# Six weight buffers at six start addresses, and the high weights of two contraction blocks multiplied first

## The chip, the cores and the metric

The kernel runs on one core of one Trainium2 chip. The metric is the device time of one execution in microseconds (us); 899.43 us is the median of two runs before the change (899.22 and 899.65). One execution was also taken with the hardware profiler, and all durations below come from it.

## The reference

A decoder trunk of two layers over 256 positions with a model width of 2048, all in float32. What matters for the time are its large projections:

```python
def ab_layer(h, w_in, gla_w_gate, gla_b_gate, gla_norm_g, w_out):
    z = h @ w_in                                  # 2048 x 7184
    ...                                           # dilated attention, 8 heads; gated linear attention, 4 heads
    y = jnp.concatenate([ya, yb], axis=-1) * jax.nn.silu(gate)
    return y @ w_out                              # 2048 x 2048

def cd_layer(h, w_in, ...):
    z = h @ w_in                                  # 2048 x 6144
    yc = s5_mixer(...)                            # state space, with y * sigmoid(y @ w_glu + b_glu), 1024 x 1024
    ...                                           # gated recurrence, 8 heads
    y = jnp.concatenate([yc, yd], axis=-1) * jax.nn.silu(gate)
    return y @ w_out                              # 2048 x 2048

for l in range(2):
    h = h + layer(rmsnorm(h, norm_g[l]))          # ab_layer, then cd_layer
return rmsnorm(h, final_g)
```

## The kernel before

**Splitting.** Each float32 operand of a projection is split into a high part, rounded to the matrix engine's reduced form (float32r), and a low part, the remainder. A product is then three products: high weights with high activations, high weights with low activations, low weights with high activations. The activations of a layer's input stand in `xh` and `xl` (2048 x 256 as 16 blocks of 128 rows), those ahead of an output projection in `yh` and `yl`.

**Weights.** All weights stream through once. `load_split` (line 143) fetches a group of four contraction blocks by 512 columns, 1 MB, into one of three `raw` buffers over SP's DMA queue. Each half of it, a pair of contraction blocks, is split: ScalarE (ACT) writes `wh` (line 168), VectorE (DVE) writes `wl` as raw minus wh (line 169). `wh` and `wl` have three buffers each, and each buffer holds one pair, 4,096 bytes per partition. Both operations are marked urgent, so the scheduler puts them ahead of the other work of their engines.

**Products.** `gemm_fm` (line 173) gives the result with features on the partitions: a weight block of 128 x 128 is loaded into the array (the stationary operand), and 256 activation columns are streamed past it (the moving operand); four such matmuls for the four column blocks of the weights, at line 181. `gemm_tm` (line 192) gives it with positions on the partitions: 128 activation columns are stationary, 512 weight columns are moving, two matmuls, at line 200. Both accumulate over 16 contraction blocks in `pg` in PSUM, and both go block by block: for one contraction block all three products, then the next block. The last quarter of the last projection has a loop of its own (line 756) over the same kind of buffers.

**Order.** The program gives the order in which work is recorded; a scheduler orders each engine's instructions at build time by a simulated timeline and priorities. It puts the product with the low activations second, ahead of the one with the low weights. Small matmuls of the attention and the recurrences are set between those of the projections; `hook` (line 134) puts pieces of the state-space layer behind the matmuls of a pair.

**Addresses.** Tiles are laid out in the order of their pools and sizes. `ones`, a small constant, is taken 56 columns wider than it is used, which moves everything behind it in memory.

Of the kernel before, what the change touches and what calls it, by code (L numbers as in the profile page):

```python
# [12 lines left out]
F32 = mybir.dt.float32  # L13
F32R = mybir.dt.float32r
# [6 lines left out]
S = 256  # L21
# [36 lines left out]
def trunk(ctx: ExitStack, tc: tile.TileContext, I, out):  # L58
    nc = tc.nc
    V, G, A, T = nc.vector, nc.gpsimd, nc.scalar, nc.tensor  # L60

    const = ctx.enter_context(tc.tile_pool(name="const", bufs=1))
    stream = ctx.enter_context(tc.tile_pool(name="stream", bufs=6))
# [8 lines left out]
    def urgent():  # L72
        return tc.high_priority(offset=HI)
# [6 lines left out]
    oT = const.tile([128, KT, S], F32, name="oT")  # L80
    cst = const.tile([128, NCST], F32, name="cst")
    msk = const.tile([128, len(LV), 32], I32, name="msk")
    ones = const.tile([128, 128 + 56], F32, name="ones")[:, 0:128]
    sqa = const.tile([128, 4, S], F32, name="sqa")
    ident = cst[:, C_ID:C_ID + 128]

# [3 lines left out]
    def pm_tile(name="pm"):  # L90
        return pm.tile([128, 512], F32, name=name, tag="pm")
# [40 lines left out]
    state = {"mm": None, "wh": None, "first": True}  # L132
    fillq = []

    def hook():
        if fillq:
            todo = fillq.pop(0)
            if todo:
                with tc.issue_after(state["mm"].ins):
                    for fn in todo:  # L140
                        fn()

    def load_split(src, g):
        raw = stream.tile([128, 4, 512], F32, name="raw", bufs=3)
        first = state["first"]
        state["first"] = first and g < 3
        with urgent():
            if first:
                for a, b in ((0, 1), (1, 2), (2, 3), (3, 4)) if g == 0 else ((0, 2), (2, 4)):
                    xs = slice(NV + (4 * g + a) * S if g + a else 0, NV + (4 * g + b) * S)  # L150
                    load(xv[:, xs], I["xv"][:, xs])
                    for c in (slice(0, 256), slice(256, 512)) if g + a == 0 else (slice(0, 512),):
                        load(raw[:, a:b, c], src[g][:, a:b, c])
                for kt in range(4 * g, 4 * g + 4):
                    split_x(kt, V_NG0)
            else:
                state["load"] = nc.sync.dma_start(raw, src[g])
        if first and g == 3:
            load_consts()
        for half in range(2):  # L160
            wh = stream.tile([128, 2, 512], F32R, name="wh", bufs=3)
            wl = stream.tile([128, 2, 512], F32R, name="wl", bufs=3)
            with urgent():
                for a, b, c, d in (((0, 1, 0, 256), (0, 1, 256, 512), (1, 2, 0, 512)) if first and g == 0
                                   else ((0, 2, 0, 512),)):
                    r = raw[:, 2 * half + a:2 * half + b, c:d]
                    w, l = wh[:, a:b, c:d], wl[:, a:b, c:d]
                    state["wh"] = A.activation(w, r, AF.Copy)  # L168
                    V.tensor_sub(l, r, w)  # L169
            for k in range(2):  # L170
                yield 4 * g + 2 * half + k, wh[:, k], wl[:, k]
            hook()

    def gemm_fm(src, groups, ah, al, mid=None, order=None):
        ps = pg.tile([128, 4, S], F32, name="pg")
        last = groups * 4 - 1
        for i, kt, wh, wl in _iter(src, groups, mid, order):
            for n, (w, a) in enumerate(((wh, ah), (wh, al), (wl, ah))):
                for c in range(4):
                    cs = slice(c * 128, (c + 1) * 128)  # L180
                    state["mm"] = T.matmul(ps[:, c], w[:, cs], a[:, kt],  # L181
                                           start=(i == 0 and n == 0 and c % 2 == 0),
                                           stop=(i == last and n == 2), skip_group_check=True)
        return ps

    def _iter(src, groups, mid, order):
        for n, g in enumerate(order or range(groups)):
            for m, (kt, wh, wl) in enumerate(load_split(src, g)):
                yield 4 * n + m, kt, wh, wl
            if mid and 2 * (n + 1) == groups:  # L190
                mid()

    def gemm_tm(src, groups, ah, al, mid=None, order=None):
        ps = pg.tile([128, 2, 512], F32, name="pg")
        last = groups * 4 - 1
        for i, kt, wh, wl in _iter(src, groups, mid, order):
            for n, (w, a) in enumerate(((wh, ah), (wh, al), (wl, ah))):
                for t in range(2):
                    ts_ = slice(t * 128, (t + 1) * 128)
                    state["mm"] = T.matmul(ps[:, t], a[:, kt, ts_], w, start=(i == 0 and n == 0),  # L200
                                           stop=(i == last and n == 2), skip_group_check=True)
        return ps

    def split_x(kt, go):
# [35 lines left out]
    f, q, k = gla_tiles()  # L240
# [135 lines left out]
    for h0 in range(0, 4, 2):  # L376
        ps = pm_tile().rearrange("p (n s) -> p n s", n=2)
# [160 lines left out]
    sp_ = sp.enter_context(tc.tile_pool(name="s5", bufs=1))  # L538
# [3 lines left out]
    for b in range(2):  # L542
        ps = gemm_fm(w1[b], 4, xh, xl)
# [8 lines left out]
    def s5_quarter(qt):  # L552
        t = {}
# [75 lines left out]
            return go  # L629

        def finish():
            ys = sp_.tile([128, 8, 64], F32, name="ys")
            A.activation(ys, t["py"], AF.Copy)
            for g in range(2):
                for s in range(4):
                    (nc.gpsimd if s % 2 else nc.scalar).dma_start(
                        yv[g, s][:, 8 * qt:8 * qt + 8], ys[g * 64 + s * 16:g * 64 + s * 16 + 16])
            yc = sp_.tile([128, 2, S], F32, name="yc")
            nc.gpsimd.dma_start(yc, s5_y[256 * qt:256 * qt + 256].rearrange("(j p) f -> p j f", p=128))
            gw = sp_.tile([128, 2, S], F32, name="gw")  # L640
            A.activation(gw, yc, AF.Square)
            A.activation(gw, gw, AF.Copy, scale=0.044715, bias=1.0)
            V.tensor_mul(gw, gw, yc)
            A.activation(gw, gw, AF.Tanh, scale=math.sqrt(2.0 / math.pi))
            A.activation(yc, yc, AF.Copy, scale=0.5)
            for n in range(2):
                V.scalar_tensor_tensor(oT[:, 2 * qt + n].rearrange("p (c s) -> p s c", s=4),
                                       gw[:, n].rearrange("p (s c) -> p s c", s=4), 1.0,
                                       yc[:, n].rearrange("p (s c) -> p s c", s=4), op0=OP.add, op1=OP.mult)
# [11 lines left out]
    for half in range(2):  # L661
        f, q, k = gla_tiles()
# [24 lines left out]
    for b in range(2):  # L687
        ps = gemm_fm(I["wg"][b], 2, yh[:, 8:16], yl[:, 8:16])
# [35 lines left out]
    part = const.tile([128, 2], F32, name="part")  # L724
# [18 lines left out]
    for b in range(3):  # L743
        res, h2 = residual(b)
        ps = gemm_tm(I["wo1"][b], 4, yh, yl, order=(2, 3, 0, 1))
# [4 lines left out]
    for half in range(2):  # L750
        ps = pg.tile([128, 2, 512], F32, name="pg")

        def mms(kt, t, w, l):
            ts_ = slice(t * 128, (t + 1) * 128)
            for n, (w_, a_) in enumerate(((w, yh), (w, yl), (l, yh))):
                T.matmul(ps[:, t, 0:256], a_[:, kt, ts_], w_, start=(kt == 0 and n == 0),  # L756
                         stop=(kt == KT - 1 and n == 2), skip_group_check=True)

        for g in range(2):
            raw = stream.tile([128, 8, 256], F32, name="raw", bufs=3)  # L760
            with urgent():
                nc.sync.dma_start(raw, I["wo1l"][half, g])
            for n in range(2):
                k0 = 8 * g + 4 * n
                if half:
                    w, l = xh[:, k0:k0 + 4], xl[:, k0:k0 + 4]
                else:
                    w = stream.tile([128, 4, 256], F32R, name="wh", bufs=3)
                    l = stream.tile([128, 4, 256], F32R, name="wl", bufs=3)
                with urgent():  # L770
                    A.activation(w, raw[:, 4 * n:4 * n + 4], AF.Copy)
                    V.tensor_sub(l, raw[:, 4 * n:4 * n + 4], w)
                for k in range(4):
                    for t in range(1 if half else 2):
                        mms(k0 + k, t, w[:, k], l[:, k])
        if half:
            for t in range(2):
                if t:
                    for kt in range(KT):
                        mms(kt, 1, xh[:, kt], xl[:, kt])  # L780
                with urgent():
                    add_in(res, h2, 3, 256, 256, t, ps[:, t, 0:256], 4)
                    store(t)
        else:
            with urgent():
                for t in range(2):
                    add_in(res, h2, 3, 0, 256, t, ps[:, t, 0:256], 3)
                presum()
# [348 lines left out]
```

## Time and profile before

| | |
|---|---|
| median of the runs | 899.43 us |
| the profiled execution, its own time | 898.85 us |
| its span, first to last instruction | 897.0 us |
| granted TensorE clock, mean | 0.996 |
| PE busy | 880.9 us, 98% |
| PE weight loads (PEld) | 806.7 us, 90% |
| DVE / ACT / POOL busy | 71% / 53% / 6% |
| mean DMA rate | 201 GB/s |
| share of PE in the chain that ended last | 88% |

A matmul's recorded duration holds its way through the array, so the durations of neighbours overlap, and a busy PE can still be a slow one. What one matmul costs in a row of them is therefore read from the chain of waits: there a piece such as "PE pg L181 x384" has the time that the row of 384 took, and time by count is the pace. "PEld" is the load of the stationary operand, which overlaps the matmul ahead of it.

### The profile page before, as it was taken

What the parts mean: (1) busy time and instruction counts of PE and PEld (TensorE: products, weight loads), DVE (VectorE), ACT (ScalarE), POOL (GpSimd) and SP (SyncE); (2) the same over time, 40 slices, a digit from 0 to 9 for tenths busy, and PEclk for the clock granted to TensorE, in tenths of its full rate; (3) what the DMA queues carried; (4) which work ended last, traced back from release to release, by engine and by line L of the source; (5) the groups of instructions that cost most, each with busy time, mean ns of one, the idle gap of its engine ahead of it and who ended that gap; (6) DMA issues with size and microseconds to landing.
All of it is one profiled execution on the core that took longest, in us unless ns stands there. A gap on an engine that the chain in (4) does not pass through costs nothing.

```text
span 897.0 us, 18689 instructions
## 1 busy us (share of the span) xinstructions
PE 880.9 (98%) x7728; PEld 806.7 (90%) x7728; DVE 636.2 (71%) x1197; ACT 472.5 (53%) x715; POOL 54.4 (6%) x106
## 2 busy tenths in 40 slices
PE   8999999999999999999999999999999999999995
PEld 8987799889998899999999998799877899988894
DVE  7987975889869758756575677776987756665562
ACT  7654546665746756544443335455455475544451
POOL 0001100111101001000000001100110000000000
PEclk9999999999999999999999999999999999999998
DMA  9837744777667546544476665754654554554532
GB/s 317 317 100 213 255 164 143 235 254 236 230 210 257 188 168 230 192 176 177 176 277 225 218 245 188 247 191 165 224 165 152 190 189 175 200 180 172 176 132 94
DMA packets 40388, 180.40 MB, mean 201 GB/s; under 512 B 12720, under 2 KB 14256, under 8 KB 22768
## 3 DMA queue, kind: packets, MB, share of 16 engines
q1 hardware_dynamic: 29440, 154.99, 49.0%
q0 software_dynamic: 7984, 22.69, 7.8%
q10 hardware_dynamic: 2880, 1.54, 0.6%
q8 instruction: 60, 0.98, 0.4%
q14 instruction: 24, 0.20, 0.1%
HBM read 166.48 MB, written 12.71 MB: 200 GB/s over the span
## 4 chain that ended last, share of the span: by engine, by line
PE 88%; DVE 4%; DMA 2%; ACT 2%; issue 2%; SPq 0%; POOL 0%; POOLq 0%; DVEq 0%
PE pg L181 51%; PE pg L200 26%; PE pg L756 2%; PE pm L287 1%; PE pm L339 1%; PE pm L621 1%; DMA E<-ed 1%; PE pm L625 1%; DVE wl L169 1%; DMA raw<-in_w_dram 1%; PE pm L583 1%; PE pm L308 1%; PE pm L415 1%; PE pm L1025 1%; ACT wh L168 1%
## 5 line engine op out<-in xcount | busy, mean ns | idle before, releaser
L168 ACT ACTIVATE wh<-raw 128x1024 fp32r<-128x1024 f32 (+2 forms) x276 | 287.7, 1045 | 324.8 <-PE pg L181 192.4
L169 DVE TENSOR_TENSOR wl<-raw,wh 128x1024 fp32r<-128x1024 f32 (+2 forms) x276 | 332.3, 1206 | 171.5 <-ACT wh L168 166.6
L181 PE MATMUL pg<-xh,wh 128*128 128x256 f32 x1024 | 161.8, 279 | 2.3 <-ACT wh L168 2.3
L181 PE MATMUL pg<-xh,wl 128*128 128x256 f32 x1024 | 163.1, 280 | 0.1
L181 PE MATMUL pg<-xl,wh 128*128 128x256 f32 x1024 | 161.1, 278 | 0.0
L181 PEld LDWEIGHTS pg<-xh,wh 128*128 128x128 f32 x1024 | 136.6, 188 | 4.0 <-ACT wh L168 3.4
L181 PEld LDWEIGHTS pg<-xh,wl 128*128 128x128 f32 x1024 | 136.9, 188 | 1.3 <-DVE wl L169 0.5
L181 PEld LDWEIGHTS pg<-xl,wh 128*128 128x128 f32 x1024 | 136.7, 188 | 0.6 <-issue 0.3
L200 PE MATMUL pg<-wl,xh 128*128 128x512 f32 x320 | 101.0, 396 | 0.7 <-DVE wl L169 0.5
L200 PE MATMUL pg<-wh,xl 128*128 128x512 f32 x320 | 100.7, 394 | 0.0
L200 PE MATMUL pg<-wh,xh 128*128 128x512 f32 x320 | 100.3, 394 | 0.0
L200 PEld LDWEIGHTS pg<-wl,xh 128*128 128x128 f32 x320 | 59.1, 188 | 14.2 <-DVE wl L169 1.6
L200 PEld LDWEIGHTS pg<-wh,xl 128*128 128x128 f32 x320 | 59.8, 188 | 12.9
L200 PEld LDWEIGHTS pg<-wh,xh 128*128 128x128 f32 x320 | 59.3, 188 | 12.8
L181 PE MATMUL pg<-yh,wh 128*128 128x256 f32 x320 | 51.8, 283 | 0.0
L181 PE MATMUL pg<-yh,wl 128*128 128x256 f32 x320 | 51.3, 282 | 0.0
L181 PE MATMUL pg<-yl,wh 128*128 128x256 f32 x320 | 51.3, 282 | 0.0
L181 PEld LDWEIGHTS pg<-yh,wh 128*128 128x128 f32 x320 | 44.1, 191 | 0.0
L181 PEld LDWEIGHTS pg<-yl,wh 128*128 128x128 f32 x320 | 44.0, 191 | 0.0
L181 PEld LDWEIGHTS pg<-yh,wl 128*128 128x128 f32 x320 | 44.0, 191 | 0.0
L965 POOL DMA_DIRECT2D tabs<-pc x44 | 23.8, 546 | 164.9 <-DVE x L975 43.3
L200 PE MATMUL pg<-wh,yh 128*128 128x512 f32 x96 | 30.4, 397 | 0.0
(350 smaller groups left out, 1008.4 us busy)
## 6 DMA issues: line engine op xcount, KB each, us to landing
raw<-in_w_dram SPq DMA_DIRECT2D x100, 1024.0 KB, 4.9
raw<-in_wo_dram SPq DMA_DIRECT2D x28, 1024.0 KB, 4.8
tb<-tabs POOLq DMA_DIRECT2D x8, 768.0 KB, 6.5
tabs<-pc POOLq DMA_DIRECT2D x20, 256.0 KB, 5.4
raw<-in_wg_dram SPq DMA_DIRECT2D x4, 1024.0 KB, 4.8
raw<-in_wo1l_dram SPq DMA_DIRECT2D x4, 1024.0 KB, 4.8
raw<-in_w_dram SPq DMA_DIRECT2D x6, 512.0 KB, 7.5
tabs<-pc POOLq DMA_DIRECT2D x24, 128.0 KB, 4.5
```

The lines of the kernel that those rows point to most:

```text
L168: state["wh"] = A.activation(w, r, AF.Copy)
L169: V.tensor_sub(l, r, w)
L181: state["mm"] = T.matmul(ps[:, c], w[:, cs], a[:, kt], start=(i == 0 and n == 0 and c % 2 == 0), stop=(i == last and n == 2), skip_group_c ...
L200: state["mm"] = T.matmul(ps[:, t], a[:, kt, ts_], w, start=(i == 0 and n == 0), stop=(i == last and n == 2), skip_group_check=True)
L287: T.matmul(ps[32 * b:32 * b + 32, t, hd], k[:, hd, r], Q[:, hd, r], start=True, stop=True)
L308: T.matmul(ps[j0:j0 + h, hd, j0 + h:j0 + 2 * h], k[:, hd, b:b + h], Qp[:, hd, b + h:b + 2 * h], start=True, stop=True)
L339: T.matmul(ps[:, (hd - h0) * dv:(hd - h0 + 1) * dv], AT[:, hd, t + j], v[:, j, hd * dv:(hd + 1) * dv], start=(j == 0), stop=(j == t))
L415: T.matmul(ps[:, t, 0:n], q[:, t * 128:(t + 1) * 128], k[:, 0:n], start=True, stop=True)
L583: T.matmul(pv[g * 64:g * 64 + 64, w, pr], t["W"][w][us, 4 * h + pr], X[us, g, 4 * h + pr], start=True, stop=True)
L621: T.matmul(py[g * 64:g * 64 + 64, pr], w[:, pr], X[:, g, pr], start=(pr == 0), stop=False, skip_group_check=True)
L756: T.matmul(ps[:, t, 0:256], a_[:, kt, ts_], w_, start=(kt == 0 and n == 0), stop=(kt == KT - 1 and n == 2), skip_group_check=True)
L965: nc.gpsimd.dma_start(tabs[qt, dst, n], t[src].rearrange("p a b -> p (a b)"))
```

## The change

It has three parts.

**Addresses.** The buffers of `wh` are made 16 columns (64 bytes) larger than what they hold, those of `wl` 32 columns (128 bytes), and `ones` is widened by 120 columns instead of 56. The used part of each buffer is the same 1,024 columns. The start addresses in the built programs, in bytes per partition, taken modulo 512:

| tile | before | after |
|---|---|---|
| xh, xl | 0, 0 | 0, 0 |
| wh, three buffers | 320, 320, 320 | 64, 128, 192 |
| wl, three buffers | 320, 320, 320 | 256, 384, 0 |
| raw, three buffers | 320 each | 64 each |
| yh, yl of the first layer | 64, 64 | 384, 384 |
| yh, yl of the second layer | 128, 128 | 448, 448 |

The blocks inside a tile are 512, 1,024 or 2,048 bytes apart, so each block of a tile has the tile's value.

**Order of the products.** `load_split` hands out a pair of contraction blocks at once, and `_iter` goes over the pair product by product: high weights with high activations for both blocks, high weights with low activations for both, low weights with high activations for both. The very first pairs of the program (first projection, first group) still go block by block.

**Room.** `ys` and `gw` of the state-space layer now share a buffer.

```diff
-    ones = const.tile([128, 128 + 56], F32, name="ones")[:, 0:128]
+    ones = const.tile([128, 128 + 120], F32, name="ones")[:, 0:128]
...
+    def split_pair(n):
+        return [stream.tile([128, 1024 + pad], F32R, name=name, bufs=3)[:, 0:1024].rearrange("p (k n) -> p k n", n=n)
+                for name, pad in (("wh", 16), ("wl", 32))]
...
-            wh = stream.tile([128, 2, 512], F32R, name="wh", bufs=3)
-            wl = stream.tile([128, 2, 512], F32R, name="wl", bufs=3)
+            wh, wl = split_pair(512)
...
-            for k in range(2):
-                yield 4 * g + 2 * half + k, wh[:, k], wl[:, k]
+            ks = [(4 * g + 2 * half + k, wh[:, k], wl[:, k]) for k in range(2)]
+            for part in ([ks[:1], ks[1:]] if first and g == 0 else [ks]):
+                yield part
             hook()
...
-    def _iter(src, groups, mid, order):
+    def _iter(src, groups, ah, al, mid, order):
+        done = 0
         for n, g in enumerate(order or range(groups)):
-            for m, (kt, wh, wl) in enumerate(load_split(src, g)):
-                yield 4 * n + m, kt, wh, wl
+            for part in load_split(src, g):
+                for w_, a in ((1, ah), (1, al), (2, ah)):
+                    for x in part:
+                        yield a, x[0], x[w_], done == 0, done == 12 * groups - 1
+                        done += 1
...
     def gemm_tm(src, groups, ah, al, mid=None, order=None):
         ps = pg.tile([128, 2, 512], F32, name="pg")
-        last = groups * 4 - 1
-        for i, kt, wh, wl in _iter(src, groups, mid, order):
-            for n, (w, a) in enumerate(((wh, ah), (wh, al), (wl, ah))):
-                for t in range(2):
-                    ts_ = slice(t * 128, (t + 1) * 128)
-                    state["mm"] = T.matmul(ps[:, t], a[:, kt, ts_], w, start=(i == 0 and n == 0),
-                                           stop=(i == last and n == 2), skip_group_check=True)
+        for a, kt, w, begin, end in _iter(src, groups, ah, al, mid, order):
+            for t in range(2):
+                ts_ = slice(t * 128, (t + 1) * 128)
+                state["mm"] = T.matmul(ps[:, t], a[:, kt, ts_], w, start=begin, stop=end, skip_group_check=True)
         return ps
...
-            ys = sp_.tile([128, 8, 64], F32, name="ys")
+            ys = sp_.tile([128, 8, 64], F32, name="ys", tag="ysgw")
...
-            gw = sp_.tile([128, 2, S], F32, name="gw")
+            gw = sp_.tile([128, 2, S], F32, name="gw", tag="ysgw")
```

`gemm_fm` is changed as `gemm_tm` is, and the loop at line 756 takes its buffers from `split_pair(256)` with its own order kept.

PE's order in the first projection, behind the first group of weights; `pg` is the accumulator, and behind the arrow stand the activations and the weights. Before:

```order
L181 MATMUL pg<-xh,wh 128x256 x4
L181 MATMUL pg<-xl,wh 128x256 x4
L181 MATMUL pg<-xh,wl 128x256 x4
L181 MATMUL pg<-xh,wh 128x256 x4
L181 MATMUL pg<-xl,wh 128x256 x4
L181 MATMUL pg<-xh,wl 128x256 x4
```

After:

```order
L183 MATMUL pg<-xh,wh 128x256 x8
L183 MATMUL pg<-xl,wh 128x256 x8
L183 MATMUL pg<-xh,wl 128x256 x8
L183 MATMUL pg<-xh,wh 128x256 x8
L183 MATMUL pg<-xl,wh 128x256 x8
```

The first matmul with low weights of a pair had 8 matmuls ahead of it in its pair and now has 16; the last one with high weights was the 20th of the pair's 24 and is now the 16th.

PE's order where the first projection with positions on the partitions begins. Before:

```order
L200 MATMUL pg<-wh,xh 128x512 x2
L200 MATMUL pg<-wh,xl 128x512 x2
L200 MATMUL pg<-wl,xh 128x512 x2
L200 MATMUL pg<-wh,xh 128x512 x2
L200 MATMUL pg<-wh,xl 128x512 x2
```

After:

```order
L203 MATMUL pg<-wh,xh 128x512 x4
L203 MATMUL pg<-wh,xl 128x512 x4
L203 MATMUL pg<-wl,xh 128x512 x4
L203 MATMUL pg<-wh,xh 128x512 x4
L203 MATMUL pg<-wh,xl 128x512 x4
```

Four matmuls stood ahead of the first low one of a pair here, and now eight do. On ACT, DVE and SP the same instructions stand as before, and some of them a few places earlier or later; on POOL nothing moves.

More of the change, by code (lines that the diff above doesn't have):

```diff
@@ L175, in gemm_fm @@
         ps = pg.tile([128, 4, S], F32, name="pg")
-        last = groups * 4 - 1
-        for i, kt, wh, wl in _iter(src, groups, mid, order):
-            for n, (w, a) in enumerate(((wh, ah), (wh, al), (wl, ah))):
[L179 to L182, printed above, removed]
-                                           stop=(i == last and n == 2), skip_group_check=True)
-        return ps
-    def _iter(src, groups, mid, order):
+        for a, kt, w, begin, end in _iter(src, groups, ah, al, mid, order):
+            for c in range(4):
+                cs = slice(c * 128, (c + 1) * 128)
+                state["mm"] = T.matmul(ps[:, c], w[:, cs], a[:, kt], start=(begin and c % 2 == 0), stop=end,
+                                       skip_group_check=True)
+        return ps
+    def _iter(src, groups, ah, al, mid, order):
+        done = 0
         for n, g in enumerate(order or range(groups)):
-            for m, (kt, wh, wl) in enumerate(load_split(src, g)):
-                yield 4 * n + m, kt, wh, wl
+            for part in load_split(src, g):
[3 more added lines that the diff above has]
+                        done += 1
             if mid and 2 * (n + 1) == groups:
@@ L194, in gemm_tm @@
         ps = pg.tile([128, 2, 512], F32, name="pg")
-        last = groups * 4 - 1
-        for i, kt, wh, wl in _iter(src, groups, mid, order):
-            for n, (w, a) in enumerate(((wh, ah), (wh, al), (wl, ah))):
-                for t in range(2):
-                    ts_ = slice(t * 128, (t + 1) * 128)
-                    state["mm"] = T.matmul(ps[:, t], a[:, kt, ts_], w, start=(i == 0 and n == 0),
-                                           stop=(i == last and n == 2), skip_group_check=True)
+        for a, kt, w, begin, end in _iter(src, groups, ah, al, mid, order):
+            for t in range(2):
+                ts_ = slice(t * 128, (t + 1) * 128)
+                state["mm"] = T.matmul(ps[:, t], a[:, kt, ts_], w, start=begin, stop=end, skip_group_check=True)
         return ps
@@ L767, in trunk @@
                 else:
-                    w = stream.tile([128, 4, 256], F32R, name="wh", bufs=3)
-                    l = stream.tile([128, 4, 256], F32R, name="wl", bufs=3)
+                    w, l = split_pair(256)
                 with urgent():
```

## The prediction

> **What bounds the kernel now.** I read the page's head and busy times first, then the groups of instructions.
>
> ```profile
> span 897.0 us, 18689 instructions
> PE 880.9 (98%) x7728; PEld 806.7 (90%) x7728; DVE 636.2 (71%) x1197; ACT 472.5 (53%) x715; POOL 54.4 (6%) x106
> PE 88%; DVE 4%; DMA 2%; ACT 2%; issue 2%; SPq 0%; POOL 0%; POOLq 0%; DVEq 0%
> L181 PE MATMUL pg<-xh,wh 128*128 128x256 f32 x1024 | 161.8, 279 | 2.3 <-ACT wh L168 2.3
> L181 PE MATMUL pg<-yh,wh 128*128 128x256 f32 x320 | 51.8, 283 | 0.0
> L200 PE MATMUL pg<-wh,xh 128*128 128x512 f32 x320 | 100.3, 394 | 0.0
> L200 PE MATMUL pg<-wh,yh 128*128 128x512 f32 x96 | 30.4, 397 | 0.0
> ```
>
> PE is busy for 98% of the span, and the big groups hardly wait. Each row stands for three products: 3 x 1024 = 3,072 matmuls of 256 columns on xh and xl; 3 x 320 = 960 on yh and yl (768 in layer one's output projection, 192 in the small projection of the state-space layer); 3 x 320 = 960 and 3 x 96 = 288 of 512 columns. What matters is how fast PE steps from one to the next. That is read from the chain of waits, which gives rows of matmuls with their time and count. On xh and xl (whole chain, then one window of it):
>
> ```profile
> 14.36 16.61 PE pg L181 x144
> 152.58 12.58 PE pg L181 x109
> 214.09 15.22 PE pg L181 x134
> 234.26 10.45 PE pg L181 x92
> 472.82 35.83 PE pg L181 x316
> 513.75 19.25 PE pg L181 x168
> 623.70 11.56 PE pg L181 x100
> 748.93 43.54 PE pg L181 x384
> ...
> 32.90 5.18 PE pg L181 x44
> ```
>
> The best rows run at 43.54 / 384 = 113.4 ns a matmul. The last row is a slower state of the same instructions, 117.7 ns; PE falls into it in some stretches. The eight rows above it sum to 165.04 us for 1,447 matmuls: 114.1 ns on average. Now the other operands: yh of layer one, the small projection with yh of layer two, and the two kinds of 512-column matmuls (first on xh, then on yh), each from the chain in its window:
>
> ```profile
> 360.89 91.66 PE pg L181 x764
> 360.89 23.14 PE pg L181 x193
> 727.51 19.55 PE pg L181 x166
> 165.16 31.12 PE pg L200 x136
> 793.35 22.41 PE pg L200 x96
> ```
>
> The same matmul of line 181 takes 91.66 / 764 = 120.0 ns on yh of layer one and 117.8 ns in the small projection. The 512-column form takes 228.8 ns on xh and 233.4 ns on yh. The shapes are equal; the start addresses differ. Other engines aren't the cause: in the window 360 to 453 us DVE and ACT are busy for only part of the time, yet the pace is the same from the first 193 matmuls (119.9 ns) to the end.
>
> ```profile
> 360.00:453.00 93.00, 93.00 (x778) 93.00 (x778) 56.17 (x62) 45.54 (x55) 0.00 (x0) 1.00 0.50 182
> ```
>
> I sort the paces by the distance between the two operands, stationary start minus moving start modulo 512. For 256 columns: distance 320 (0 and 320) 113.4 or 117.7 ns; 256 (yh at 64) 120.0; 192 (yh at 128) 117.8. The last loop adds two cases, yh as the stationary operand against streamed weights at 320 (distance 320), then against weights kept in xh at 0 (distance 128):
>
> ```profile
> 863.17 11.20 PE pg L756 x95
> 874.25 5.94 PE pg L756 x50
> 725.73 1.78 PE pm L339 x16
> ```
>
> They give 117.9 and 118.8 ns. So 320 is the only distance at which the quick state is seen, and not always. For 512 columns: 192 gives 228.8, 320 gives 233.4. The third row, small matmuls of 128 columns that also load 128 columns of weights each, is the lowest pace of a loading matmul that I find, 111.3 ns; I use it as a floor.
>
> The Trainium skill says otherwise: "SBUF — State Buffer", section "Who interferes with whom", gives PE two independent read ports, one for the moving operand and one for weight loads, and says that PE never waits on anyone. By that rule start addresses would cost nothing; the trace disagrees, with 113.4 against 120.0 ns for one shape.
>
> **The change part by part.** *Addresses.* The matmuls on xh keep moving start 0, and their weights go from 320 to 64, 128, 192 (wh) and 256, 384, 0 (wl): six distances, without 320. Three are seen: 128 at 118.8, 192 at 117.8, 256 at 120.0. For 64, 384 and 0 no row exists; they lie between 111.3 and 120.0 unless a distance is worse than all seen. I take 116.7, the middle of the quickest and the slowest row of line 181 (113.4 and 120.0): three of the four distances seen lie above it, but the floor lies below them all, and nothing decides between the two. wh carries two products of three: (116.7 + 118.8 + 117.8) / 3 = 117.8; wl: (120.0 + 116.7 + 116.7) / 3 = 117.8. So 114.1 becomes 117.8, 3.7 ns x 3,072 = +11.4 us.
>
> Layer one's output projection (yh at 384): wh at distances 192, 256, 320, mean (117.8 + 120.0 + 113.4) / 3 = 117.1; wl at 384, 0, 128, mean 117.4; together 117.2, so -2.8 x 768 = -2.2 us. The small projection (yh at 448): wh 118.9, wl 115.6, together 117.8, nothing. The 192 matmuls of the last loop stay within 0.2 us by the same means.
>
> In the 512-column form the activations are stationary. On xh the distances are 448, 384, 320 (wh) and 256, 128, 0 (wl). Only 320 is seen, 233.4; the rest gets 231.1, between the two rows. The mean is 231.6: +2.8 x 960 = +2.7 us. On yh at 448: wh 384, 320, 256, wl 192, 64, 448, mean 231.4: -2.0 x 288 = -0.6 us. Bounds for an unseen distance here: twice the floor, 222.6, and 233.4.
>
> Sum of the addresses: 11.4 - 2.2 + 2.7 - 0.6 = +11.3 us. ACT and DVE write the moved buffers too; should that make them slower, DVE has 29% of the span to spare.
>
> *Order.* It can only win where PE waits for wl:
>
> ```profile
> 11.99 1.07 ACT wh L168
> 13.08 1.24 DVE wl L169
> 14.36 16.61 PE pg L181 x144
> ...
> PE pg L181 <- ACT wh L168: 2.3, 3, 1.1
> PE pg L200 <- DVE wl L169: 0.5, 2, 0.3
> PEld pg L200 <- DVE wl L169: 1.6, 3, 0.8
> ```
>
> At 13 us PE has wh, runs eight matmuls (0.9 us) and waits for wl, which DVE finishes 1.24 us after it started; 16 matmuls last 1.8 us and cover it, 0.3 us. ACT's wait for the transfer ahead of it stays. The 512-column waits of 0.5 us (1.6 us by the weight loads) go too, with 1.8 us of matmuls ahead of wl instead of 0.9. I take -1.0 us, bounds 0 and -1.9. wh comes free four matmuls earlier in a pair and wl no later, so ACT and DVE start no later. If this cover were gone, PE would again wait those 1.9 us at most.
>
> *The rest.* gw on ACT now waits until the stores of ys are done; but its input yc is read back from what they store, so it waits for them anyway; 0. The loads of the state-space constants move by one or two places on SP's queue among the weight loads; three raw buffers lie between that queue and PE, whose waits for wh sum to 2.3 us in the whole run; 0.
>
> Total: 11.3 - 1.0 = +10.3 us on the profiled execution's 897.0 us span, 907.3 us, and with the 1.85 us outside the span (898.85 us its own time) 909.2 us. The median is 0.6 us above that execution: 899.4 + 10.3 = 909.7. I forecast 909 us.
>
> **The rivals.** *Neutral (chance 0.22).* What counts is the moving operand's start alone, or the six distances average to what there is now. For: all the line-181 rows have weights at 320 and differ in the moving operand. Against: with xh moving at 0, other stationary data gave 118.8 instead of 113.4, and with weights moving at 320, 233.4 instead of 228.8. The order's 1.0 us remains: 898 us. The rule of two independent ports in the Trainium skill's page "SBUF — State Buffer" gives the same. That the buffers don't move is excluded by the address table.
>
> *Gain (0.25).* Changing the distance every 8 matmuls frees PE from the slow states, and all of line 181 runs at 113.4, all of line 200 at 228.8: -0.7 x 3,072 = -2.2, -6.6 x 768 = -5.1, -4.4 x 192 = -0.8, -4.6 x 288 = -1.3, the order -1.0: 889 us. With line 200 at 222.6 (-6.2 x 1,248 = -7.7) it is 881, and with line 181 at the floor, -2.1 x 4,032 = -8.5, 873 us. For: 114.1 and 120.0 are both above the floor. Against: of four distances seen, one shows the quick state. I give 0.10 to more than 2%. The Trainium skill ("TensorE: Matmul & The Clock Gate", section "Back-to-back issue gap") has columns / 2.4 + 2.5 ns between warm matmuls, 109.2 and 215.8 ns; by it an estimated 43 us could be won in all, and 113.4 and 228.8 ns show that no row here reaches it.
>
> *Loss over 2% (0.08).* No unseen distance is better than the worst seen: 120.0 in all of line 181 on xh, 233.4 on line 200. 5.9 x 3,072 = 18.1, plus 4.6 x 960 = 4.4, plus 0.4, minus 1.0: 921 us. It decides once the matmuls on xh pass about 120 ns on average.
>
> *Forecast (0.45).* With the unseen distances at their bounds (111.3 and 222.6, or 120.0 and 233.4) and the order at its own, the same sums give -7 to +19 us, 892 to 918 us.
>
> **The numbers.** About 2%, 18 us, is what a measurement of this kernel can tell from no change: 881 to 917 us. The range of 8 in 10 leaves out the gains beyond 886 (about 0.13) and the upper part of the loss (0.07): 886 to 917. Faster by over 2%: 0.10, from the gain case; slower: 0.08; within: 0.82.
>
> **What would show it.** In the new profile the chain's long pieces of line 183 (181 before) on xh give about 118 ns a matmul and differ between wh and wl rows; on yh of layer one they fall from 120.0 to 117; line 203 goes from 229 to about 231. The waits of PE for wl at line 203 are gone. I am wrong if pieces on xh stay at 113.4, or if the pace is one for all six buffers; and wrong in kind if the time moves and the paces don't.

## The result: 2.4% slower, outside the range

The changed kernel takes 920.91 us (median of two runs, 920.21 to 921.61) against 899.43 us: 1.0237 times as long, 95% interval 1.0212 to 1.0261. The forecast was 909 us with a range of 886 to 917. The sign was right and the size was half of what came. The profiled execution has a span of 918.4 us, 21.4 us more than the one before.

The page of the changed kernel, its head and two groups (columns as in the prediction; line 181 is now line 183, 200 is 203, 168 is 171, 169 is 172):

```profile
span 918.4 us, 18702 instructions
PE 890.9 (97%) x7728; PEld 817.2 (89%) x7728; DVE 635.6 (69%) x1197; ACT 473.9 (52%) x715; POOL 54.5 (6%) x106
PE 75%; DMA 2%; issue 2%; ACT 1%; DVE 1%; POOL 0%; POOLq 0%; DVEq 0%; ACTq 0%
...
L203 PE MATMUL pg<-wh,xh 128*128 128x512 f32 x320 | 89.2, 399 | 4.3 <-ACT wh L171 4.3
...
L183 PE MATMUL pg<-yh,wh 128*128 128x256 f32 x320 | 44.8, 282 | 4.9 <-ACT yh L509 4.9
```

Two groups that never waited before now wait 4.3 and 4.9 us. The list of PE's waits shows both again, as single events, with smaller ones behind them (columns: us in total, times, longest; the list is cut):

```profile
PE pg L183 <- ACT yh L509: 4.9, 2, 2.6
PE pg L203 <- ACT wh L171: 4.3, 1, 4.3
PE pm L289 <- DVE gk L327: 2.6, 3, 1.2
PE pg L183 <- ACT wh L171: 2.3, 4, 0.9
```

Before, the longest single wait of this list was 1.1 us. The second thing to read is the pace. Pieces of the chain of waits of the changed kernel, start, duration and count, three on xh in the 256-column form, one in the small projection, two in the 512-column form (on xh, then on yh), the last loop, and from a window of its own layer one's output projection:

```profile
487.16 37.39 PE pg L183 x318
529.75 19.96 PE pg L183 x168
748.19 19.27 PE pg L183 x163
769.21 45.13 PE pg L183 x384
292.04 22.20 PE pg L203 x96
815.21 22.30 PE pg L203 x96
884.69 16.94 PE pg L758 x144
...
381.98 73.04 PE pg L183 x626
```

Time by count: 117.6, 118.8 and 117.5 ns on xh (the prediction had 117.8), 118.2 in the small projection (117.8), 231.3 and 232.3 ns in the 512-column form (231.6 and 231.4), 116.7 ns (73.04 / 626) on yh of layer one (117.2), 117.6 ns in the last loop (117.9 and 118.8 before). The paces came as forecast, to within a nanosecond or so.

To put sizes on both, I took the step from the start of one matmul of a projection to the start of the next from the trace, where no other work stands between the two. The mean of the steps up to 127 ns (256 columns) or 246 ns (512 columns), times the 5,280 matmuls, counts as pace. What longer steps have above that mean counts as stalls, those at a low clock among them. "Rest" is what the span has beyond these (matmuls of other work in between, and the ends). Differences from the kernel before, in us, each from its profiled execution; they hold to about half a microsecond:

| kernel | span | pace, 256 col. | pace, 512 col. | stalls | rest |
|---|---|---|---|---|---|
| changed kernel | +21.4 | +7.4 | +1.8 | +11.3 | +0.8 |
| addresses alone | +16.4 | +7.8 | +2.0 | +2.4 | +4.2 |
| order alone | +14.6 | +1.6 | 0.0 | +12.9 | 0.0 |

The pace gave +9.2 us where the prediction had +11.3 for the addresses. The stalls gave +11.3 us where it had -1.0 for the order. The rows "alone" are the first two experiments.

### Where the two stalls come from

ACT's timeline around 168 us, first of the kernel before, then of the changed one (start us, duration, line, operation; in brackets the idle time before it and what ended that):

```profile
160.27 3.30 ACT L351 ACTIVATE oT<-go,hrs 128x256 f32<-128x256 f32 x8
163.47 1.04 ACT L168 ACTIVATE wh<-raw 128x1024 fp32r<-128x1024 f32 x1
164.42 2.01 ACT L1055 ACTIVATE pc<-cst,m 128x64 f32<-128x64 f32 x8
166.33 1.05 ACT L168 ACTIVATE wh<-raw 128x1024 fp32r<-128x1024 f32 x1
```

```profile
159.03 1.06 ACT L171 ACTIVATE wh<-raw 128x1024 fp32r<-128x1024 f32 x1 [1.73 <-PE pg L183]
166.48 0.35 ACT L1056 ACTIVATE pc<-cst,m 128x64 f32<-128x64 f32 x1 [6.39 <-DVE x L978]
166.74 3.29 ACT L353 ACTIVATE oT<-go,hrs 128x256 f32<-128x256 f32 x8
169.93 1.76 ACT L1056 ACTIVATE pc<-cst,m 128x64 f32<-128x64 f32 x7
171.60 1.99 ACT L171 ACTIVATE wh<-raw 128x1024 fp32r<-128x1024 f32 x2
```

Before, the weight splits stand between the two batches of other work. After, the first of the eight operations that write a decay table of the state-space layer (line 1056) stands ahead of them. It waits 6.39 us for the preparation's own work (the trace names DVE's line 978), the eight `oT` and the other seven table operations follow, and only then come two weight splits. ACT goes through all of these without a pause, and from 168 us no transfer is under way (DMA share 0.00 in the window below), so the two splits waited only for the instructions ahead of them. From the end of the split at 160.1 us to the next one at 171.6 us PE gets no new wh; it runs dry at 168.

The wait has a tail. Windows of the changed kernel (168 to 173 and 173 to 178 us), and of the kernel before just behind its own splits; columns are us, busy time and count of PE, PEld, DVE, ACT, POOL, then the granted TensorE clock, DMA share and GB/s:

```profile
168.00:173.00 5.00, 0.67 (x3) 0.31 (x2) 0.33 (x1) 5.00 (x15) 0.54 (x1) 0.81 0.00 2
173.00:178.00 5.00, 5.00 (x13) 3.87 (x13) 5.00 (x7) 3.07 (x4) 0.00 (x0) 0.51 0.70 257
```

```profile
170.00:175.00 5.00, 5.00 (x23) 4.11 (x22) 2.71 (x4) 2.12 (x2) 0.00 (x0) 1.00 0.99 336
```

In the 5 us behind the wait the granted clock is 0.51 and 13 matmuls run, where 23 ran before: 10 x 0.23 = 2.3 us on top of the 4.3.

The second stall is on another path. The tables of the state-space layer are written to memory by POOL; yh and yl of layer one take memory that the buffers of this preparation give back, so ACT may write yh only when the last table has left. The last puts on POOL's timeline, before and after:

```profile
351.94 0.54 POOL L965 DMA_DIRECT2D tabs<-pc  x1 [5.68 <-DVE pc L978]
353.40 0.54 POOL L965 DMA_DIRECT2D tabs<-pc  x1 [0.92 <-DVE pc L979]
```

```profile
364.61 0.57 POOL L966 DMA_DIRECT2D tabs<-pc  x1 [5.92 <-ACT pc L1056]
366.33 1.08 POOL L966 DMA_DIRECT2D tabs<-pc  x2 [1.15 <-DVE pc L979]
```

The last table is put 13 us later, although POOL has its instructions in the order of before: what writes the tables is late. The last quarter of the preparation begins with 32 small matmuls on PE, and these start 15 us later. The lines of all 128 such matmuls, before and after, with their durations in ns and then the first and the last start:

```profile
L1025 PE MATMUL pm<-PP,bb x128: 221/222/271, 151.4 to 333.8; 128*64 128x64 f32 x128
```

```profile
L1026 PE MATMUL pm<-PP,bb x128: 222/222/270, 149.9 to 348.8; 128*64 128x64 f32 x128
```

In the trace 1,892 matmuls of the projections stood ahead of the last 32, and now 1,943 do; at some 117 ns each these 51 places are 6 us. The other 9 are the delay that PE has by then. PE itself comes to yh only 10 us later, at 370.7 us instead of 360.7.

The transfer of the last table also takes longer, 5.37 us against some 3.3 (from the put at 353.4 to 356.7). Before, ACT began with yh when that transfer landed, 4 us ahead of PE's first matmul on it, as ACT's and PE's timelines show:

```profile
356.77 1.57 ACT L507 ACTIVATE yh<-pm,xv 128x256 fp32r<-128x256 f32 x4 [0.67 <-DMA tabs<-pc]
```

```profile
360.73 0.63 PE L181 MATMUL pg<-yh,wh 128*128 128x256 f32 x4
```

After, ACT begins at 372.5 us and PE, through with the matmuls ahead, has already waited since 370.7. In the chain of the window 340 to 382 us of the changed kernel it is followed through to PE:

```profile
366.87 5.37 DMA tabs<-pc
...
372.50 1.57 ACT yh L509 x4
```

Here too the clock is low behind the wait (0.67 from 376 to 381 us). ACT's order and the place of the small matmuls on PE were changed by the scheduler at build time, as a consequence of the new order of the large matmuls; no line of the diff touches lines 353, 509, 1026 or 1056.

### The profile page after: what moved, and what is told of

Its sections match the earlier page's. It is cut to its first block, busy times and chain, and to the rows that moved or that the text cites. A ratio compares the mean times of both kernels' runs of the same rounds, so it can differ in the third digit from the quotient of the medians.

```text
span 918.4 us, 18702 instructions
## 1 busy us (share of the span) xinstructions
PE 890.9 (97%) x7728; PEld 817.2 (89%) x7728; DVE 635.6 (69%) x1197; ACT 473.9 (52%) x715; POOL 54.5 (6%) x106
## 4 chain that ended last, share of the span: by engine, by line
PE 75%; DMA 2%; issue 2%; ACT 1%; DVE 1%; POOL 0%; POOLq 0%; DVEq 0%; ACTq 0%
PE pg L183 39%; PE pg L203 27%; PE pg L758 2%; PE pm L623 1%; PE pm L585 1%; PE pm L627 1%; PE pm L289 1%; PE pm L417 1%; DMA s5y<-ys 1%; DMA tabs<-pc 1%; PE pm L341 1%; DMA yc<-s5y 0%; PE pm L310 0%; PE pm L1026 0%; PE pm L714 0%
## 5 line engine op out<-in xcount | busy, mean ns | idle before, releaser
L183 PE MATMUL pg<-xh,wl 128*128 128x256 f32 x1024 | 146.5, 284 | 0.0
L183 PE MATMUL pg<-xl,wh 128*128 128x256 f32 x1024 | 145.3, 282 | 0.0
L183 PE MATMUL pg<-xh,wh 128*128 128x256 f32 x1024 | 142.6, 281 | 2.3 <-ACT wh L171 2.3
L183 PEld LDWEIGHTS pg<-xh,wh 128*128 128x128 f32 x1024 | 129.3, 188 | 4.0 <-ACT wh L171 3.1
L183 PEld LDWEIGHTS pg<-xl,wh 128*128 128x128 f32 x1024 | 130.1, 188 | 0.5
L203 PE MATMUL pg<-wh,xh 128*128 128x512 f32 x320 | 89.2, 399 | 4.3 <-ACT wh L171 4.3
L203 PE MATMUL pg<-wh,xl 128*128 128x512 f32 x320 | 89.3, 399 | 0.0
L203 PE MATMUL pg<-wl,xh 128*128 128x512 f32 x320 | 89.2, 398 | 0.0
L183 PE MATMUL pg<-yh,wh 128*128 128x256 f32 x320 | 44.8, 282 | 4.9 <-ACT yh L509 4.9
L183 PE MATMUL pg<-yh,wl 128*128 128x256 f32 x320 | 44.5, 281 | 0.0
```

The costliest lines, as they stand in the source:

```text
L183: state["mm"] = T.matmul(ps[:, c], w[:, cs], a[:, kt], start=(begin and c % 2 == 0), stop=end, skip_group_check=True)
L203: state["mm"] = T.matmul(ps[:, t], a[:, kt, ts_], w, start=begin, stop=end, skip_group_check=True)
```

## The experiments

My theory after the result: two independent costs, the distance between the operands (+9 us) and the changed order of ACT and of the preparation of the tables (+11 us). The rivals: that the new addresses alone cause all of it (the stalls being a consequence of a slower PE), and, on the pace, that what counts is the moving operand's own start.

### Each part alone

Addresses alone, in the kernel before; every engine's instructions stand in the order of before:

```diff
-    ones = const.tile([128, 128 + 56], F32, name="ones")[:, 0:128]
+    ones = const.tile([128, 128 + 120], F32, name="ones")[:, 0:128]
...
-            wh = stream.tile([128, 2, 512], F32R, name="wh", bufs=3)
-            wl = stream.tile([128, 2, 512], F32R, name="wl", bufs=3)
+            wh, wl = split_pair(512)
```

(and the same in the last loop, with `ys` and `gw` in one buffer)

> The new start addresses with the old order of the products; every engine's instructions stand as in the kernel before. Two causes (the address part costs about 10 us in pace, the new order about 11 us in two stalls near 168 and 370 us): 909 us, chain pieces on xh at about 117 ns a matmul, no PE wait for wh over 1.5 us and no wait for yh. All from the addresses: 920 us, with both stalls. All from the order: 899 us.

Measured: 910.5 us, 1.0106 times the kernel before (1.0063 to 1.0149). The pace takes +9.8 us, as in the changed kernel; neither of the two stalls is there. Its profiled execution is the longest of its runs (span 913.4 us) and has two waits of its own, this one and one of 2.3 us of a small matmul for `gk` (its part of the rest):

```profile
PE pg L203 <- DVE wl L172: 2.9, 2, 2.6
```

So the new paces can tip a wait even in the old order, but it is not one of the two.

Order alone, in the changed kernel with the old addresses; every engine's instructions stand in the order of the changed kernel:

```diff
-    ones = const.tile([128, 128 + 120], F32, name="ones")[:, 0:128]
+    ones = const.tile([128, 128 + 56], F32, name="ones")[:, 0:128]
...
-                for name, pad in (("wh", 16), ("wl", 32))]
+                for name, pad in (("wh", 0), ("wl", 0))]
```

(and `ys` and `gw` with a buffer each)

> The new order of the products with the old start addresses; every engine's instructions stand as in the changed kernel. Two causes: 910 us, pieces on xh at 114 ns and on yh of layer one at 120 ns as before, and both stalls there (a PE wait for wh of over 4 us near 165 us, and a wait for yh of some 5 us near 365 us). All from the addresses: 899 us or a little less. All from the order: 920 us.

Measured: 914.0 us, 1.0171 (1.0123 to 1.0219). The pace is that of before, and both stalls are there in full:

```profile
PE pg L183 <- ACT yh L509: 5.2, 2, 3.1
PE pg L203 <- ACT wh L171: 4.8, 1, 4.8
```

The order that was to win 1 us costs 14.6 us (11 to 20 by the interval). This settles the first question: the stalls belong to the order, the paces to the addresses. The two parts sum to 11.1 + 14.6 = 25.7 us, more than the 21.5 us of both together; with intervals of 4 us to each side on each part, that is no contradiction.

### Taking the stalls away

In the order-alone kernel I removed what makes the two instructions late. For the first, the decay tables go to DVE; for the second, the last pieces of the state-space preparation are recorded ahead of the second attention's heads. First both together:

```diff
-                A.activation(dk[:, r_], cst[:, C_RM:C_RM + 64], AF.Copy, scale=m4[:, 8 * qt + r_:8 * qt + r_ + 1])
+                V.tensor_scalar(dk[:, r_], cst[:, C_RM:C_RM + 64], m4[:, 8 * qt + r_:8 * qt + r_ + 1], None, op0=OP.mult)
```

```diff
-    heads(qk1, 6)
     for _ in prep:
         pass
+    heads(qk1, 6)
```

> The new order with the old start addresses, and two edits against the two stalls: the decay table of the state-space preparation (8 small operations a quarter) is made on DVE instead of ACT, so that no weight split queues behind it on ACT, and the last quarter of that preparation is recorded ahead of the last two attention heads, so that its tables leave earlier. If these queues are the cause of the order's loss: 897 to 899 us, neither stall in the profile. If the order of the products itself is slow: about 910 us still.

Measured: 904.88 us, 1.0063 (1.0039 to 1.0088). Both stalls are gone, and 9 of the 14.6 us came back, not all. The list of waits, from a profiled execution that at 909.09 us is 4 us above the median, shows that waits have moved:

```profile
PE pm L289 <- DVE gk L327: 4.1, 3, 2.4
PE pm L433 <- DVE pr L430: 2.9, 1, 2.9
PE pg L183 <- ACT wh L171: 2.6, 3, 1.9
PE pg L203 <- DVE wl L172: 1.9, 2, 1.6
```

I missed by 6 to 8 us, having summed the two waits as if nothing stood behind them. Each edit by itself tells them apart. The decay tables on DVE alone (the first of the two edits):

> The new order with the old addresses, and only the decay tables moved from ACT to DVE. Theory (each stall is a cost of its own, set by what is queued ahead of the weight split): the wait of PE for ACT's wh at line 203 near 168 us, 4.8 us with the order alone, goes, and with it the slow stretch behind it, some 3 us; the wait for ACT's yh at line 509 (5.2 us) stays. 914.0 - 4.8 - 3 = 906 us. Rival (what goes at one place comes back at another, since the scheduler orders all engines anew): 910 us or more, with new waits of PE in the list.

Measured: 913.26 us, 1.0156 (1.0133 to 1.0178), as long as the order alone within the intervals: my theory falls for this stall, the rival holds. The wait of 4.8 us at line 203 is gone from the list, and so is the slow clock behind it (24 matmuls at 1.00):

```profile
173.00:178.00 5.00, 5.00 (x24) 4.10 (x23) 5.00 (x8) 2.12 (x2) 1.07 (x2) 1.00 0.77 262
```

But others are there in its place:

```profile
PE pm L289 <- DVE gk L327: 3.5, 3, 1.6
PE pm L433 <- DVE pr L430: 3.3, 2, 2.3
```

Stalls within the projections fell by 4.8 us against the order alone, and the rest, in which the waits of the small matmuls between them count, rose by 4.6. The tables now stand on DVE, where `gk` of the gated linear attention and `pr` of the attention come from; and with an operation moved, the scheduler orders all engines anew. Which of the two delays `gk` and `pr` I have not separated.

The preparation earlier, alone (the second edit):

> The new order with the old addresses, and only the last pieces of the state-space preparation recorded ahead of the attention heads. Theory (each stall is a cost of its own): the last table is put before 360 us, the wait of PE for ACT's yh at line 509 near 367 us, 5.2 us with the order alone, goes with what follows it; the wait at line 203 near 168 us (4.8 us) stays. 914.0 - 5.2 - 1 = 908 us. Rival (what goes at one place comes back at another): 911 us or more.

Measured: 908.38 us, 1.0105 (1.0077 to 1.0133), as the theory had it (908). The last tables are put at 337 us instead of 366, and no wait for yh is left; the wait at line 203 stays (4.7 us):

```profile
337.31 1.08 POOL L966 DMA_DIRECT2D tabs<-pc  x2 [3.29 <-DVE pc L979]
```

So of the order's 14.6 us, some 6 are the late tables, by removing them alone (914.0 against 908.4 us, with intervals that overlap a little). The wait behind the decay tables may be worth another 3 or 4 us when the tables are early (908.4 against 904.9 us; these intervals overlap a little too), and nothing that can be measured without that. Some 5 us remain. By the list of waits they lie in smaller ones, mostly for `gk` and `pr` from DVE; I have not undone these one by one, so this part is not shown.

### The distance

Four experiments on the kernel before, with its order. First yh and yl at 0 instead of 64 and 128, so that the distance is 320 wherever weights are stationary:

```diff
-        pT = ap_.tile([128, 384 + 8], F32, name="pT", bufs=1)[:, 0:384]
+        pT = ap_.tile([128, 384 + 8 + 112], F32, name="pT", bufs=1)[:, 0:384]
...
-    zs2 = [gate_tm(w1[10 + n], rc1, gz.tile([128, 4 * S + 24 * n], F32, name=f"gz{n}")[:, 0:4 * S]
+    zs2 = [gate_tm(w1[10 + n], rc1, gz.tile([128, 4 * S + 120 * n], F32, name=f"gz{n}")[:, 0:4 * S]
```

> The kernel before with yh and yl of both layers moved from 64 and 128 to start address 0 modulo 512, so that their distance to the weights is 320 as that of xh is; order unchanged. If the distance between stationary and moving start sets the pace: layer one's output projection goes from 120.0 to 113.4 ns a matmul (-5 us), the small projection from 117.8 to 113.4 (-0.8), the 512-column matmuls on yh from 233.4 to 229 (-1.3): 892 us. If start addresses only seem to matter: 899 us.

Measured: 892.97 us, 0.9926 (0.9904 to 0.9947). This is quicker than both kernels, and as expected (892). Layer one's output projection from the window 365 to 450 us, and the 512-column form on yh:

```profile
364.97 85.11 PE pg L181 x751
...
787.07 21.98 PE pg L200 x96
```

85.11 / 751 = 113.3 ns instead of 120.0, and 229.0 ns instead of 233.4.

Second, everything 64 bytes on (xh to 64, weights to 384, yh to 128 and 192), with all distances as they were:

```diff
-    xv = const.tile([128, NV + KT * S], F32, name="xv")
+    xv = const.tile([128, NV + KT * S + 16], F32, name="xv")[:, 0:NV + KT * S]
```

> The kernel before with every tile behind the input moved by 64 bytes: xh and xl begin at 64 instead of 0 modulo 512, the weights at 384, yh at 128 and 192. All distances between stationary and moving start stay as they were (320, 256, 192). If the distance sets the pace: 899 us, 113.4 ns on xh, 120.0 on yh of layer one. If the moving operand's own start sets it (0 is quick, 64 is slow): 120 ns on xh, some 918 us.

Measured: 898.79 us, 0.9986 (0.9971 to 1.0002). The paces are those of before, 43.54 us for 384 matmuls on xh and 80.04 for 667 on yh of layer one (120.0 ns):

```profile
749.29 43.54 PE pg L181 x384
...
369.97 80.04 PE pg L181 x667
```

A move of all starts with the distances kept changes nothing, so the moving operand's own start is not what counts. This takes away what stood for the neutral rival.

Third and fourth, weights at 0 (distance 0) and at 448, both with yh and yl at 0, by the width of `ones` and of the two tiles padded above:

```diff
-    ones = const.tile([128, 128 + 56], F32, name="ones")[:, 0:128]
+    ones = const.tile([128, 128 + 104], F32, name="ones")[:, 0:128]
```

> The kernel before with all six weight buffers at 0 modulo 512, and yh, yl of both layers at 0 too: distance 0 everywhere, in the old order. If the distance counts modulo 256, it is the case of yh in layer one before (256): 120 ns on line 181 throughout, so about +6 x 3,072 = +18 us, +0.4 in the small projection, 918 us, about as slow as the changed kernel without any stall. If a distance is only bad when the buffers differ: 899 us.

Measured: 912.68 us, 1.0147 (1.013 to 1.0165). Line 181 runs at 120.0 ns throughout, but line 200 got quicker, 227.0 ns on yh, which I had not expected. Some 3 us of the 5 by which the time stays under 918 come from there:

```profile
761.53 46.08 PE pg L181 x384
808.48 21.79 PE pg L200 x96
```

and with 88 columns in place of 104:

> The kernel before with all six weight buffers at 448 modulo 512, and yh, yl of both layers at 0: distance 448 for line 181, 64 for line 200, which no run has had in one piece. If the distance counts modulo 256, 448 is as 192, which ran at 113.4 ns in parts of the changed kernel: 893 us, as with yh at 0 and the weights at 320. If only distance 320 is quick: 118 ns, 905 us or more.

Measured: 915.61 us, 1.0173 (1.0151 to 1.0194):

```profile
764.26 45.23 PE pg L181 x384
810.37 22.40 PE pg L200 x96
```

45.23 / 384 = 117.8 ns for line 181, 233.3 for line 200. That fits the second expectation (118 ns, 905 us or more). Sorted as above, some 12 of the 16 us are pace; the others are waits. At 448 the first form does not take the pace that a distance of 192 mostly has in the changed kernel (114.1 ns), but the 117.8 ns that 192 has in the small projection of before. So a reading of the distance by 256 bytes instead of 512 did not foretell the time; with two states to a distance it is not excluded either.

## Why the prediction was wrong

**The failed step is "Order", "I take -1.0 us, bounds 0 and -1.9".** It measured +14.6 us alone, and +11.3 us of stalls within the changed kernel. The step priced what the large matmuls do with the new order, and asked only whether wl comes in time. It then said that "wh comes free four matmuls earlier in a pair and wl no later, so ACT and DVE start no later". That is true of a single pair, and not of the queue: the split that PE needed at 168 us stood on ACT behind an instruction that waited 6.39 us, and yh came late at 370 us because the tables were. The bound "if this cover were gone, PE would again wait those 1.9 us at most" was made from waits for wl alone. That a wait on ACT ahead of a split holds up the splits behind it could be suspected from the trace of before (there the splits stand between batches of 3.30 and 2.01 us); and the changed order of ACT, and of the small matmuls on PE, stood in the built program before the run. I read the change for the large matmuls and for SP, and put ACT's order and the preparation of the tables at nothing.

**Addresses: mechanism right, the sum nearly right and in part by luck, +9.2 for +11.3 us.** The 11.4 us on xh and -2.2 on yh are +7.4 together in the sorted steps (+9.2 forecast), and the 512-column terms +1.8 (+2.1). Taking 116.7 and 231.1 ns for unseen distances, the middle of what was seen, was good enough for the sum: 64 came at 116.4 ns and 384 at 118.3, while 0 was as slow as 256 (119.8) and 192, seen at 117.8, ran at 114.1 on xh. So wh and wl, forecast alike at 117.8, came at (116.4 + 118.6 + 114.1) / 3 = 116.4 and (119.6 + 118.3 + 119.8) / 3 = 119.2 ns; the misses cancel in part, which is luck. That paces follow the distance was an inference from rows that all had weights at 320; the move by 64 bytes shows it.

**"The rest", 0.** The order-alone kernel has `ys` and `gw` apart and the new order of SP, and its paces and waits are explained without either. Nothing points to a cost here.

**The rivals.** The loss case has almost the measured time (921 us), by another mechanism: it had 120.0 ns on all of xh and 233.4 at line 203 throughout. The paces stayed at 116.7 to 118.8, so its chance was not the one that came true. The gain case needed the alternation to free PE from the slow states; of the six buffers in the changed kernel only the one at 192 came near the quick state on xh (114.1 ns). The neutral case needed the distance not to matter; yh at 0 speaks against it, with 113.3 instead of 120.0 ns, and the move by 64 bytes shows that it is not the start alone. The Trainium skill's page "SBUF — State Buffer", section "Who interferes with whom", gives PE two independent read ports; these paces don't agree with that as far as start addresses go. What I lacked was a rival with its place on ACT or in the preparation of the tables: "a split comes late because of what is queued ahead of it". The prices of two such waits stood ready in the rows of before, a batch of `oT` (3.30 us) and one of tables (2.01 us) ahead of a split that PE needs.

**The signs I named.** "About 118 ns" on xh, 117 on yh of layer one, about 231 at line 203: all came. "The waits of PE for wl at line 203 are gone": they are, and a wait for wh of 4.3 us stands there. "Wrong in kind if the time moves and the paces don't" is what the order alone shows: 14.6 us with the old paces.

## What to carry to other kernels

When a change reorders the work of the busiest engine under a build-time scheduler, read the new order of every engine's queue, the small matmuls on the busiest one among them, and for each instruction that waits look at what is queued behind it and who needs that; on an engine with half its time to spare, one waiting instruction ahead of a weight split made PE wait 4.3 us here. The distance between the start of the stationary and of the moving operand is worth a sweep of its own, over all operands and both forms of matmul: 892.97 us came from padding two small tiles. And the length of a wait is not the gain from removing it: 4.8 us of waiting, moved away with its cause to another engine, gave nothing that could be measured, and 5.2 us removed by earlier tables gave some 5.6, its slow stretch included.

## What the runs showed that I had not expected

**Distance has no single best value.** With stationary start minus moving start modulo 512:

| distance | 256 columns, ns | 512 columns, ns |
|---|---|---|
| 0 | 119.9 (weights at 0, 4,116 steps) | 227.6 (weights at 0, 1,186) |
| 64 | 116.4 (changed, 632); 113.4 (weights at 448, last loop, 94) | 233.3 (weights at 448, 1,175) |
| 128 | 118.6 (changed, 723) | 232.0 (changed, 75) |
| 192 | 117.8 (before, 187); 114.1 (changed, 832) | 229.2 (before, 902) |
| 256 | 120.0 (before, 767) | 231.1 (changed, 132) |
| 320 | 114.1 (before, 3,057) | 233.3 (before, 282) |
| 384 | 118.3 (changed, 361) | 232.4 (changed, 236) |
| 448 | 117.4 (weights at 448, 3,892) | 230.5 (changed, 208) |

These are means of the pace steps between two matmuls of the same distance, with the kernel and their count. The two forms want opposite things: 0 is among the slowest of one and the quickest of the other. One distance can also run in two states, 113.4 and 117.8 ns at 320 and at 192, each kept for whole stretches; what decides between them stays open, and so does the cause of the distance's effect.

**A pause can cost more than its own length.** After 4.7 us without a matmul, from start to start, the changed kernel's granted clock was 0.50 for the next 5.2 us. The Trainium skill ("TensorE: Matmul & The Clock Gate", section "Part 1: The HAM clock gate (the "warmup" mystery)") has the clock fall to half after an idle window of about 3.4 us and return after as much work. The fall agrees with that; the return took 5.2 us of work here. But shorter pauses brought the clock down too, and not always. With the addresses alone, a single pause of 2.8 us at 92 us was followed by

```profile
97.00:102.00 5.00, 5.00 (x18) 3.96 (x17) 4.96 (x7) 2.01 (x2) 0.02 (x1) 0.77 0.98 305
```

and with the weights at 448 one of 1.9 us at the same place by 0.79 in the same window, whereas 2.2 us at 168 us, in the kernel with the tables on DVE, left it at 1.00. So the length of a pause alone does not tell whether the clock falls here; what decides stays open.
